# Loading the first token blocks and weights by halves in the start of a hybrid decoder layer

## The chip, the core and the metric

The kernel runs on one core of one Trainium2 chip. Its time is the device time of one execution in microseconds; lower is better. A time is given as the median of several runs, and one further execution is profiled.

## The reference

One layer of a decoder trunk on a sequence of 512 tokens, 1024 channels, in float32. Cut to what matters:

```python
u = rmsnorm(x, norm1_g)
proj = u @ w_in            # -> a_glu, q, k, v, r, g_low, gate_a, gate_b
y_conv = silu(layernorm(dwconv31(glu(a_glu)))) @ w_conv_out
y_gla = (gated_linear_attention(q, k, v, g_low) * silu(r)) @ w_gla_out
h = x + (sigmoid(gate_a) * y_conv + sigmoid(gate_b) * y_gla) @ w_o
u2 = rmsnorm(h, norm2_g)
z = dwconv3(u2 @ w_ffn_up)
h = h + (silu(z[:, :F]) * z[:, F:]) @ w_ffn_down
return rmsnorm(h, final_g)
```

The case plays in the first line and in the first product of the second one: the RMS norm of x and the first 512 of the 1024 columns of v.

## The kernel before, in words

**Products in three parts.** A float32 product is made of three products of TensorE on numbers cast to a shorter form (fp32r). Each operand is split: its high part is a cast on ScalarE, its low part is the operand less the high part, on VectorE. Of the four products of parts, the kernel makes high by high (HH), high weight by low activation (HL) and low weight by high activation (LH), and adds them up in one bank of PSUM. `mm3` (L305) does so for most of the kernel, at L309 to L311; `by_parts` (L512, product at L519) does so in the start, where the three parts can be asked for one by one.

**Tiles.** x comes in four token blocks of 128 x 1024 (x0 to x3). The weights come as blocks of 128 x 1024, 512 KB each. For v a weight block holds two steps k of the inner dimension (rows), each with 512 columns; so the first half of the columns of block w0 is step 0, its second half is step 1. A product of the start has 128 tokens of one step k as the stationary operand and the 512 columns of one half of a weight block as the moving one. One token block needs eight steps by three parts, 24 products, in one bank.

**The start (L409 to L598).** It stands under `manual_schedule`, so TensorE, ScalarE, VectorE and SyncE each do their instructions in exactly the order of the code. For the first two token blocks (`EARLY = 2`) the norm is not applied ahead of the product: `transposed` turns x to channels by tokens with four transposes per half of the columns (L433), `with_gain` multiplies by the norm's gain on VectorE (L439), `early_high` casts on ScalarE (L446) and `early_low` subtracts on VectorE (L449). The factor of each token is applied to the result (L502). `squares` (L453) sums the squares of a token block on ScalarE. The gain itself comes as `rows`, is turned by TensorE (L525) and copied by VectorE (L526). `split_weight(True)` (L259, L262) gives high and low of a weight block as two halves each, `split_weight()` (L266, L267) in one piece. `warm(n)` (L425) issues n dummy products of 128 x 128 that nobody reads; each is two instructions in the trace. `WARM` says how many stand in each of three places: before the first transposes, before the first product, and after the first six products.

**Order before the change.** SyncE issues: gain rows, x0, w0, x1, w1, w2, x2, w3, all in one piece. TensorE: 7 dummies, transposes of x0, 3 dummies, HH of block 0 on steps 0 and 1, the eight transposes of x1, HL and LH of block 0 on steps 0 and 1, 2 dummies, then HH and HL of block 0 on steps 2 and 3 (which need w1), HH of block 1 on steps 0 and 1, and so on. ScalarE casts both halves of w1 ahead of the first half of block 1. VectorE makes the gain of block 1's second half late, after the lows of w1 and of block 0's second half.

**Behind the start** (from `load_consts`, L133) the order is not written out: the framework's planner orders instructions by the order of the code, by dependencies and by its own estimates of costs, and the depthwise convolution's taps are dealt out between the products by `fill`. Weight blocks come through four buffers (`raw`, L174), each split to high and low and used by the products. The other stages are the same in both versions: GLU and convolution, attention, the merge, w_o, and the feed-forward part.

Of the kernel before, what the change touches and what calls it, by code (L numbers as in the profile page):

```python
# [10 lines left out]
F32 = mybir.dt.float32  # L11
# [6 lines left out]
P = 128  # L18
D = 1024
T = 512  # L20
# [14 lines left out]
AHEAD = 4  # L35
LOOK = 2
RATE = 5.0
WARM = (7, 3, 2)
MID = 4
EARLY = 2  # L40
PADS = (416, 2016, 640)
# [25 lines left out]
def trunk_layer(ctx: ExitStack, tc: tile.TileContext, a: dict, out: bass.AP):  # L67
    nc = tc.nc

    def pool(name, bufs, space=None):  # L70
        kw = {"space": space} if space is not None else {}
        return ctx.enter_context(tc.tile_pool(name=name, bufs=bufs, **kw))
# [10 lines left out]
    tp = pool("temps", 1)  # L83
# [8 lines left out]
    def nm(s):  # L92
        return f"{s}_{next(names)}"

    def heap(dt=F32):
        return hp.tile([P, T], dt, tag="h", name=nm("h"))
# [65 lines left out]
    ready, raws = [], []  # L162
# [4 lines left out]
    def load():  # L167
        if len(raws) < len(order):
            name, j = order[len(raws)]
            if name in SEVEN:  # L170
                raws.append(load_block(name, *j))
                return
            raw = raw_tile()
            nc.sync.dma_start(raw, a[name][j])  # L174
            raws.append(raw)

    def raw_tile():
        return wp.tile([P, D], F32, tag="raw", name=nm("raw"), bufs=4)
# [16 lines left out]
    def load_block(name, pairs, step, d):  # L195

        if step not in LOADS:
            return None
        src = block(name, pairs, d, *LOADS[step])
        n = src.shape[-1]  # L200
        if step == "a11":
            dst = keep_tile(name)[:, :n]
            kept[pairs, d] = dst
        else:
            dst = raw_tile()[:, :n]
        nc.sync.dma_start(dst, src)
        if step == "n3":
            nc.gpsimd.dma_start(dst, block(name, pairs, d, 1, 1), accum_op=ALU.add)
        if step == "n2":
            kept[pairs, d, "b22"] = dst  # L210
        return dst

    def operand(raw, pairs, step, d):

        if step == "s4":
            return kept[pairs, d, "b22"]
        if step == "n2":
            nc.vector.tensor_tensor(kept[pairs, d], kept[pairs, d], raw, ALU.add)
        return raw if step in ("a12", "n3") else kept[pairs, d]

    def sum_on(name, pairs, step, d):

        if step in ("a11", "n2"):
            nxt = block(name, pairs, d, *((0, 1) if step == "a11" else (1, 0)))
            nc.gpsimd.dma_start(kept[pairs, d], nxt, accum_op=ALU.add)

    def split_weight(halves=False, between=None):

        if len(ready) < len(order):
            while len(raws) <= len(ready):  # L230
                load()
            raw = raws[len(ready)]
            name, spec = order[len(ready)]
            if name in SEVEN:
                raw = operand(raw, *spec)
                n = raw.shape[-1]
                hi = wp.tile([P, D], F32R, tag="whi", name=nm("whi"), bufs=4)[:, :n]
                lo = wp.tile([P, D], F32R, tag="wlo", name=nm("wlo"), bufs=4)[:, :n]
                nc.scalar.copy(hi, raw)  # L239
                nc.vector.tensor_tensor(lo, raw, hi.bitcast(F32), ALU.subtract)  # L240
                sum_on(name, *spec)
                ready.append((hi, lo))
                load()
                return
            hi = wp.tile([P, D], F32R, tag="whi", name=nm("whi"), bufs=4)
            if order[len(ready)][0] == "w_low":
                nc.scalar.copy(hi, raw)
                if order[len(ready)][1] == 0:
                    part_lo = lambda t: t.rearrange("p (k c) -> p k c", c=P)[:, :, :RANK]
                    nc.vector.tensor_tensor(part_lo(hi), part_lo(raw), part_lo(hi.bitcast(F32)), ALU.subtract)  # L250
                ready.append((hi, None))
                load()
                return
            lo = wp.tile([P, D], F32R, tag="wlo", name=nm("wlo"), bufs=4)
            if halves:
                ready.append((hi, lo))

                def high(c):
                    nc.scalar.copy(hi[:, c], raw[:, c])  # L259

                def low(c):
                    nc.vector.tensor_tensor(lo[:, c], raw[:, c], hi[:, c].bitcast(F32), ALU.subtract)  # L262

                cols = [slice(j * T, (j + 1) * T) for j in range(2)]
                return [[lambda c=c, part=part: part(c) for c in cols] for part in (high, low)]
            nc.scalar.copy(hi, raw)  # L266
            pace[0] = nc.vector.tensor_tensor(lo, raw, hi.bitcast(F32), ALU.subtract)  # L267
            ready.append((hi, lo))
            load()
# [130 lines left out]
    xs, rs, xg, eu = {}, {}, {}, {}  # L400

    def load_x(t):
        xs[t] = tp.tile([P, D], F32, tag="x", name=nm("x"), bufs=3)
        nc.sync.dma_start(xs[t], a["x"][t * P : (t + 1) * P, :])

    def by_four(t):
        return t.rearrange("p (k t) -> p k t", k=4)
# [2 lines left out]
    start.__enter__()  # L410
    rows = tp.tile([P, P], F32, tag="gain", name=nm("rows"), bufs=1)[0:KT, :]
    nc.sync.dma_start(rows, a["norm1_g"].rearrange("(k p) -> k p", p=P))
    load_x(0)
    load()
    load_x(1)
    load()
    load()
    load_x(2)
# [17 lines left out]
    def with_gain(tr, g):  # L436
        f = heap()
        by_channel = gains[:, g * 4 : g * 4 + 4].unsqueeze(2).to_broadcast([P, 4, P])
        nc.vector.tensor_tensor(by_four(f), by_four(tr), by_channel, ALU.mult)  # L439
        return f  # L440
# [4 lines left out]
    def high(hi, f):  # L445
        nc.scalar.copy(hi, f)  # L446

    def low(lo, f, hi):
        nc.vector.tensor_tensor(lo, f, hi.bitcast(F32), ALU.subtract)  # L449
# [16 lines left out]
    def early_gain(t, g):  # L466
        xg[t, g] = with_gain(xg[t, g], g)
        eu[t, g] = [by_four(heap(F32R)) for _ in range(2)]

    def early_high(t, g):  # L470
        high(eu[t, g][0], by_four(xg[t, g]))

    def early_low(t, g):
        low(eu[t, g][1], by_four(xg[t, g]), eu[t, g][0])
# [35 lines left out]
    HH, HL, LH = (0, 0), (0, 1), (1, 0)  # L510

    def by_parts(acc, t, ks, parts=(HH, HL, LH)):  # L512

        for wi, ai in parts:
            for k in ks:
                act = eu[t, k // 4][ai][:, k % 4, :] if t < EARLY else acts1[k][ai][:, t * P : (t + 1) * P]
                j = slice((k % 2) * T, (k % 2 + 1) * T)
                first, last = k == 0 and (wi, ai) == HH, k == KT - 1 and (wi, ai) == LH
                nc.tensor.matmul(acc, act, ready[k // 2][wi][:, j], start=first, stop=last)  # L519

    accs = [mm_bank() for _ in range(EARLY)]
    warm(WARM[0])
    xg[0, 0] = transposed(xs[0], 0)
# [6 lines left out]
    highs, lows = split_weight(True)  # L530
    highs[0]()
    early_high(0, 0)
    highs[1]()
    warm(WARM[1])
    lows[0]()
    early_low(0, 0)
    lows[1]()
    by_parts(accs[0], 0, (0, 1), (HH,))
    early_acts(1)
    squares(0)  # L540
    by_parts(accs[0], 0, (0, 1), (HL, LH))
    warm(WARM[2])
    early_gain(1, 0)
    highs, lows = split_weight(True)
    for half in (*highs, *lows):
        half()
    early_high(1, 0)
    load()
    early_low(1, 0)
    early_high(0, 1)  # L550
    by_parts(accs[0], 0, (2, 3), (HH, HL))
    by_parts(accs[1], 1, (0, 1), (HH,))
    by_parts(accs[0], 0, (2, 3), (LH,))
    by_parts(accs[1], 1, (0, 1), (HL, LH))
    by_parts(accs[1], 1, (2, 3))
    early_low(0, 1)
    early_gain(1, 1)
    split_weight()
    load_x(3)
    early_high(1, 1)  # L560
# [54 lines left out]
    for k in range(KT):  # L615
# [4 lines left out]
        c = heap()  # L620
# [504 lines left out]
    class Finish:  # L1125
# [8 lines left out]
        def part(self, n, c):  # L1134
            hn = hres[self.t, n][:, c]
            k = len(self.parts)
            nc.scalar.activation(junk(T)[:, c], hn, AF.Square, scale=1.0 / 32.0, accum_out=self.ss[:, k : k + 1])
            y = self.y[:, n * T + c.start : n * T + c.stop] if self.y else tmp() if self.parts else hn
            nc.vector.tensor_tensor(y, hn, gain3[:, n * T + c.start : n * T + c.stop], ALU.mult)
            self.parts.append((n, y))  # L1140
            self.width += c.stop - c.start
            if k == 0:
                self.sum = small(1, "var")
                nc.vector.tensor_scalar(self.sum, self.ss[:, 0:1], EPS, None, ALU.add)
            elif self.width < D:
                nc.vector.tensor_tensor(self.sum, self.sum, self.ss[:, k : k + 1], ALU.add)
# [39 lines left out]
    for gi, pairs in enumerate(GROUPS):  # L1186
        acts = []
        early = {}
        if gi == 0:

            ws = [weight("w_up", j, 0) for i in pairs[0] for j in (i, FT + i)]
            accs = [mm_bank() for _ in ws]
# [107 lines left out]
```

## Time and profile before

| | |
|---|---|
| median of 3 runs | 838.51 us (837.78 to 838.71) |
| the profiled execution's own time | 837.74 us |
| its span | 836.0 us |
| instructions | 10033 |
| moved by DMA | 97.79 MB, mean 117 GB/s |

The profile is of one execution. Its span is counted from the first instruction to the last; the time of an execution holds a little more, here 1.74 us. Times in the views are counted from the start of the span. A row of a timeline has start, length, engine, line, operation, what is written and read, and a count; in brackets stands how long the engine sat idle before and what ended it. PE is TensorE, PEld its weight load, ACT ScalarE, DVE VectorE, POOL GpSimd, SP SyncE. The matmuls are pipelined, so neighbouring rows of PE overlap. The tiles in the start: `x` token blocks, `raw` weight blocks, `whi` and `wlo` their high and low parts, `h` both the gained activations and their parts, `ax` the bank of transposes, `mm` the banks of products.

### The profile page before, as it was taken

To read this page: it belongs to the slowest core of one execution; us is meant where nothing else is said; L and a number is where in the kernel's file an instruction comes from. 1 tells how busy PE (TensorE), PEld (TensorE's weight loads), DVE (VectorE), ACT (ScalarE), POOL (GpSimd) and SP (SyncE) were. 2 spreads that over 40 slices of the span, in tenths; PEclk is the share of its full clock that TensorE was granted. 3 is DMA by queue.
4 is the path that set the end of the run, shared out by engine and by line. 5 is a ranking of instruction groups with operands and counts; after the bars stand their busy time and mean duration, and the time that the engine had idled before them with its cause. 6 is when DMAs were issued, how large, how long until landed. Compare 5 with 4: busy or idle time off the path is not lost.

```text
span 836.0 us, 10033 instructions
## 1 busy us (share of the span) xinstructions
PE 826.9 (99%) x3845; PEld 691.3 (83%) x3845; DVE 650.3 (78%) x927; ACT 388.0 (46%) x541; POOL 42.8 (5%) x64
## 2 busy tenths in 40 slices
PE   9999999999999999999999999999999999999996
PEld 7888888888888888888888898888888888888885
DVE  6689979999998798744689858778757787676795
ACT  6633247445543422449444635444434444444454
POOL 2000000000100100000001100001000010000111
PEclk9999999999999999999999999999999999999999
DMA  8232232222222322232348634234842238222462
GB/s 312 102 102 101 101 104 80 101 76 96 82 76 76 127 100 101 76 102 75 114 89 237 190 128 142 88 98 102 217 148 89 69 86 286 102 91 87 101 125 102
DMA packets 28593, 97.79 MB, mean 117 GB/s; under 512 B 3240, under 2 KB 3632, under 8 KB 28544
## 3 DMA queue, kind: packets, MB, share of 16 engines
q1 hardware_dynamic: 25088, 85.35, 29.2%
q0 software_dynamic: 3456, 11.80, 8.1%
q8 instruction: 30, 0.49, 0.2%
q14 instruction: 19, 0.16, 0.1%
HBM read 95.03 MB, written 2.10 MB: 116 GB/s over the span
## 4 chain that ended last, share of the span: by engine, by line
PE 96%; DVE 1%; DMA 1%; issue 0%; ACT 0%; POOL 0%; SPq 0%; POOLq 0%; ACTq 0%
PE mm L309 29%; PE mm L310 29%; PE mm L311 29%; PE mm L519 3%; PE ax L854 1%; PE ax L310 1%; PE ax L309 1%; PE ax L311 1%; DMA x<-in_x_dram 1%; PE ax L856 1%; PE ax L836 1%; PE ax L823 0%; PE ax L871 0%; DVE hres L1019 0%; PE ax L822 0%; PE ax L433 0%
## 5 line engine op out<-in xcount | busy, mean ns | idle before, releaser
L309 PE MATMUL mm<-uh,wlo 128*128 128x512 f32 (+1 forms) x768 | 294.8, 384 | 0.0
L311 PE MATMUL mm<-uh,whi 128*128 128x512 f32 (+1 forms) x768 | 292.4, 381 | 0.0
L310 PE MATMUL mm<-ul,whi 128*128 128x512 f32 (+1 forms) x768 | 292.2, 380 | 0.0
L266 ACT CAST whi<-raw 128x1024 fp32r<-128x1024 f32 x114 | 118.7, 1046 | 129.0 <-PE mm L311 97.2
L311 PEld LDWEIGHTS mm<-uh,whi 128*128 128x128 f32 x768 | 144.4, 188 | 27.8
L309 PEld LDWEIGHTS mm<-uh,wlo 128*128 128x128 f32 x768 | 144.5, 188 | 27.0
L310 PEld LDWEIGHTS mm<-ul,whi 128*128 128x128 f32 x768 | 144.5, 188 | 26.9
L267 DVE TENSOR_TENSOR wlo<-raw,whi 128x1024 fp32r<-128x1024 f32 x114 | 138.3, 1217 | 34.9 <-ACT whi L266 34.8
L613 DVE SCALAR_TENSOR_TENSOR c<-h,pp,c 128x511 f32<-128x511 f32 (+14 forms) x240 | 162.3, 727 | 0.7
L1083 DVE SCALAR_TENSOR_TENSOR tmp<-mm,pp,tmp 128x511 f32<-128x511 f32 x88 | 65.8, 748 | 68.1 <-ACT tmp L1081 67.0
L1081 ACT ACTIVATE tmp<-mm,pp 128x512 f32<-128x512 f32 x44 | 34.3, 780 | 62.6 <-PE mm L311 62.6
L239 ACT CAST whi<-kept 128x1024 fp32r<-128x1024 f32 (+1 forms) x32 | 31.7, 994 | 21.7 <-PE mm L311 9.7
L240 DVE TENSOR_TENSOR wlo<-kept,whi 128x1024 fp32r<-128x1024 f32 (+1 forms) x32 | 36.6, 1152 | 2.5 <-ACT whi L239 2.3
L1019 DVE TENSOR_TENSOR hres<-hres,mm 128x512 f32<-128x512 f32 (+1 forms) x49 | 32.7, 671 | 3.3 <-PE mm L311 2.7
L239 ACT CAST whi<-raw 128x1024 fp32r<-128x1024 f32 (+1 forms) x24 | 23.7, 995 | 20.2 <-PE mm L311 18.7
L240 DVE TENSOR_TENSOR wlo<-raw,whi 128x1024 fp32r<-128x1024 f32 (+1 forms) x24 | 27.3, 1152 | 3.9 <-ACT whi L239 3.8
L310 PE MATMUL mm<-wlo,sh 128*128 128x512 f32 x66 | 25.8, 391 | 0.0
L311 PE MATMUL mm<-whi,sh 128*128 128x512 f32 x66 | 25.7, 389 | 0.0
L309 PE MATMUL mm<-whi,sl 128*128 128x512 f32 x66 | 25.5, 389 | 0.0
L309 PE MATMUL mm<-h,wlo 128*128 128x512 f32 x64 | 25.4, 397 | 0.0
L310 PE MATMUL mm<-h,whi 128*128 128x512 f32 x64 | 24.9, 389 | 0.0
L311 PE MATMUL mm<-h,whi 128*128 128x512 f32 x64 | 24.9, 389 | 0.0
(251 smaller groups left out, 1122.3 us busy)
## 6 DMA issues: line engine op xcount, KB each, us to landing
raw<-in_w_up_dram SPq DMA_DIRECT2D x44, 512.0 KB, 3.5
raw<-in_w_glu_dram SPq DMA_DIRECT2D x16, 512.0 KB, 3.9
raw<-in_w_down_dram SPq DMA_DIRECT2D x15, 512.0 KB, 3.2
kept<-in_w_down_dram POOLq DMA_DIRECT2D x10, 512.0 KB, 5.2
raw<-in_w_v_dram SPq DMA_DIRECT2D x8, 512.0 KB, 3.7
raw<-in_w_qk_dram SPq DMA_DIRECT2D x8, 512.0 KB, 3.2
raw<-in_w_r_dram SPq DMA_DIRECT2D x8, 512.0 KB, 3.3
raw<-in_w_gb_dram SPq DMA_DIRECT2D x8, 512.0 KB, 3.2
```

The source lines that it names most:

```text
L239: nc.scalar.copy(hi, raw)
L240: nc.vector.tensor_tensor(lo, raw, hi.bitcast(F32), ALU.subtract)
L266: nc.scalar.copy(hi, raw)
L267: pace[0] = nc.vector.tensor_tensor(lo, raw, hi.bitcast(F32), ALU.subtract)
L309: nc.tensor.matmul(acc, ll, rh, start=first, stop=False, **kw)
L310: nc.tensor.matmul(acc, lh, rl, start=False, stop=False, **kw)
L311: nc.tensor.matmul(acc, lh, rh, start=False, stop=last, **kw)
L519: nc.tensor.matmul(acc, act, ready[k // 2][wi][:, j], start=first, stop=last)
L613: nc.vector.scalar_tensor_tensor(y[:, s:], c[:, : T - s], w, y[:, s:], ALU.mult, ALU.add)
L1019: nc.vector.tensor_tensor(hres[t, n][:, c], hres[t, n][:, c], bank[of[step]][i][:, c], op)
L1081: nc.scalar.activation(z, acc, AF.Identity, bias=pp[:, PP_FB + m : PP_FB + m + 1], scale=w[2])
L1083: nc.vector.scalar_tensor_tensor(z[:, s:], acc[:, : T - s], w[j], z[:, s:], ALU.mult, ALU.add)
```

## The change

The diff:

```diff
-WARM = (7, 3, 2)
+WARM = (5, 2, 2)
...
-    load_x(0)
-    load()
-    load_x(1)
+
+    raws.append(raw_tile())
+    for t in range(EARLY):
+        xs[t] = tp.tile([P, D], F32, tag="x", name=nm("x"), bufs=3)
+    for t, c in ((t, slice(j * T, (j + 1) * T)) for t in range(EARLY) for j in range(2)):
+        nc.sync.dma_start(xs[t][:, c], a["x"][t * P : (t + 1) * P, c])
+        if t == 0:
+            nc.sync.dma_start(raws[0][:, c], a["w_v"][0][:, c])
     load()
     load()
     load_x(2)
...
     warm(WARM[1])
-    lows[0]()
     early_low(0, 0)
-    lows[1]()
+    for half in lows:
+        half()
     by_parts(accs[0], 0, (0, 1), (HH,))
     early_acts(1)
     squares(0)
     by_parts(accs[0], 0, (0, 1), (HL, LH))
     warm(WARM[2])
     early_gain(1, 0)
+    early_gain(1, 1)
+    early_high(1, 0)
+    early_low(1, 0)
     highs, lows = split_weight(True)
     for half in (*highs, *lows):
         half()
-    early_high(1, 0)
     load()
-    early_low(1, 0)
     early_high(0, 1)
+    by_parts(accs[1], 1, (0, 1), (HH,))
     by_parts(accs[0], 0, (2, 3), (HH, HL))
-    by_parts(accs[1], 1, (0, 1), (HH,))
+    by_parts(accs[1], 1, (0, 1), (HL, LH))
     by_parts(accs[0], 0, (2, 3), (LH,))
-    by_parts(accs[1], 1, (0, 1), (HL, LH))
     by_parts(accs[1], 1, (2, 3))
     early_low(0, 1)
-    early_gain(1, 1)
     split_weight()
```

SyncE now issues x0, w0 and x1 as six transfers of half the columns each (256 KB, rows of 2 KB): first half of x0, first half of w0, second half of x0, second half of w0, then the two halves of x1; behind them w1, w2, x2 and w3 in one piece as before. In the prediction a and b stand for the first and second half (x1b is the second half of x1). The dummies become 5, 2 and 2. On VectorE the low part of block 0's first half goes ahead of both lows of w0; both gains and the first low of block 1 go ahead of the lows of w1. On ScalarE the cast of block 1's first half goes ahead of both casts of w1. On TensorE the HH of block 1 on steps 0 and 1 comes before the products of block 0 on steps 2 and 3, and its HL and LH come before block 0's LH on steps 2 and 3. The same products are made, and the same bytes are loaded.

## The prediction

> **What bounds the kernel now.** I read the page first: the span, the busy shares and the chain that ended last.
>
> ```profile
> span 836.0 us, 10033 instructions
> ...
> PE 826.9 (99%) x3845; PEld 691.3 (83%) x3845; DVE 650.3 (78%) x927; ACT 388.0 (46%) x541; POOL 42.8 (5%) x64
> ...
> PE 96%; DVE 1%; DMA 1%; issue 0%; ACT 0%; POOL 0%; SPq 0%; POOLq 0%; ACTq 0%
> ```
>
> TensorE is busy for 826.9 of 836.0 us and carries 96% of the chain. So nothing but TensorE time counts, and only 9.1 us of it are idle. The next view, busy time by stretches, says where those 9.1 us are not:
>
> ```profile
> 33.39:825.00 791.61, 791.56 (x3663) 661.73 (x3662) 622.75 (x880) 361.48 (x497) 36.55 (x42) 1.00 0.37 114
> ```
>
> From 33.39 us, where the hand-ordered start ends, to 825 us TensorE is busy for 791.56 of 791.61 us. Whatever the start saves or loses is handed through to the end undiminished, and nothing behind it can be won. The question is at which time TensorE's unbroken work begins. The chain of waits over the first 40 us answers it (columns: start, length, what):
>
> ```profile
> 2.13 6.11 DMA x<-in_x_dram
> 8.28 1.09 PE ax L433 x8
> 9.38 0.93 PE mm L519 x4
> 10.31 0.44 PE mm L425 x4
> 10.75 6.92 PE mm L519 x30
> ...
> 25.38 8.18 PE mm L519 x36
> ```
>
> The end of the kernel hangs on the landing of the second token block at 2.13 + 6.11 = 8.24 us. From there TensorE does that block's eight transposes (1.09 us), four products (0.93), four dummy products (0.44), and from 10.75 on products without a break: 6.92/30 = 0.231 us each, later 8.18/36 = 0.227. Before the landing TensorE has room to spare, as its timeline shows:
>
> ```profile
> 1.12 3.32 PE L425 MATMUL mm<-ones 128*128 128x128 f32 x14 [1.12 <-DVE ones L398]
> 4.70 0.63 PE L433 MATMUL ax<-ident,x 128*128 128x128 f32 x4 [0.26 <-DMA x<-in_x_dram]
> ...
> 5.90 0.83 PE L425 MATMUL mm<-ones 128*128 128x128 f32 x6
> 7.11 1.02 PE L519 MATMUL mm<-whi,h 128*128 128x512 f32 x2 [0.38 <-ACT h L446]
> 8.28 1.09 PE L433 MATMUL ax<-ident,x 128*128 128x128 f32 x8
> ```
>
> Each dummy of the code is two instructions. The first product starts at 7.11 us and two are done by 8.1; after that TensorE sits until x1 is there. So the time of the first product is not what the end hangs on; x1 is.
>
> **The change, part by part.**
>
> *Loads by halves.* Five transfers of 512 KB (x0, w0, x1 among them) become two whole ones and six halves of 256 KB. What does a half cost? Four rows: the page's landing times, and the packets of stretches that hold one lone transfer each (one of 256 KB in 2.0 us, one of 512 KB in 2.5 us):
>
> ```profile
> raw<-in_w_down_dram SPq DMA_DIRECT2D x15, 512.0 KB, 3.2
> raw<-in_w_down_dram SPq DMA_DIRECT2D x3, 256.0 KB, 2.5
> ```
> ```profile
> q1 hardware_dynamic: 144, 0.26, 36.6%
> ```
> ```profile
> q1 hardware_dynamic: 144, 0.52, 60.7%
> ```
>
> A lone half lands 0.7 us sooner. Its packets take 0.366 x 16 x 2.0 = 11.7 us of engine time, two halves 23.4; the whole takes 0.607 x 16 x 2.5 = 24.3. So two halves take the engines no longer than one whole. The halves cost more on SyncE's queue, which issues them one by one:
>
> ```profile
> 1.26 0.36 SPq L404 DMA_DIRECT2D x<-in_x_dram  x1
> 1.67 0.42 SPq L174 DMA_DIRECT2D raw<-in_w_v_dram  x1
> 2.13 0.43 SPq L404 DMA_DIRECT2D x<-in_x_dram  x1
> 2.60 1.01 SPq L174 DMA_DIRECT2D raw<-in_w_v_dram  x2
> ```
> ```profile
> x<-in_x_dram SPq DMA_DIRECT2D x1, 512.0 KB, 3.3
> raw<-in_w_v_dram SPq DMA_DIRECT2D x1, 512.0 KB, 4.1
> ```
>
> x0 is issued at 1.26 and lands 3.3 later, at 4.6; w0 is issued at 1.67 and lands 4.1 later, at 5.8. With 0.46 us per issue (2.13 to 2.60 and on), the order x0a, w0a, x0b, w0b, x1a, x1b puts x1's second half at 1.26 + 5 x 0.46 = 3.6 us instead of 2.13, and w1 at 4.0 instead of 2.60; everything behind them on SyncE (w2, x2, w3) is 1.4 us later too. At 3.6 us, however, four halves are still on their way: I put x0a at 1.26 + 2.5 = 3.8 us, then one half per 0.7 us, w0a 4.5, x0b 5.2, w0b 5.9 (the whole w0 was 5.8). The engines do not run dry, so x1 is complete when as many bytes as before have come: 8.24 us. Bounds: an earlier landing down to 7.3 (the spacing of 0.7 continued), and a later one by the whole delay of its issue, 1.4 us. I take 0.15 us later, near the equal-engine-time rows, for more semaphore packets and the later issue. x1a comes between, at about 7.0 to 7.6.
>
> *Fewer dummies (14 to 10 instructions, 6 to 4, 4 unchanged).* They lie before x1's landing, where TensorE waits; removing them gains nothing there. The first run ends at 1.12 + 10 x 0.237 = 3.5 us instead of 4.4.
>
> *x0's way to the first product.* From the transposes at 4.70 to the product at 7.11 are 2.4 us: transposes, two steps on VectorE, one on ScalarE.
>
> ```profile
> 5.72 1.29 DVE L439 TENSOR_TENSOR h<-ax,gains 128x512 f32<-128x512 f32 x2
> 6.92 0.68 DVE L262 TENSOR_TENSOR wlo<-raw,whi 128x512 fp32r<-128x512 f32 x1
> 7.52 0.68 DVE L449 TENSOR_TENSOR h<-h,h 128x512 fp32r<-128x512 f32 x1
> 8.12 0.68 DVE L262 TENSOR_TENSOR wlo<-raw,whi 128x512 fp32r<-128x512 f32 x1
> 8.98 0.69 DVE L439 TENSOR_TENSOR h<-ax,gains 128x512 f32<-128x512 f32 x1 [0.17 <-PE ax L433]
> ```
> ```profile
> 6.44 0.62 ACT L446 CAST h<-h 128x512 fp32r<-128x512 f32 x1
> 6.97 0.62 ACT L259 CAST whi<-raw 128x512 fp32r<-128x512 f32 x1
> 7.49 1.05 ACT L453 ACTIVATE junk<-x 128x1024 bf16<-128x1024 f32 x1
> 8.45 0.19 ACT L453 ACTIVATION_READ_ACCUMULATOR junk<-x 128x1 f32 x1
> 9.58 1.14 ACT L259 CAST whi<-raw 128x512 fp32r<-128x512 f32 x2 [0.95 <-DMA raw<-in_w_v_dram]
> ```
>
> Starting at 3.8 the first product comes at about 6.3, 0.8 sooner. That is worth nothing by itself, as TensorE then waits for x1. It lets VectorE be ahead: two gains, then three lows (0.6 us from start to start), from 4.9 to 8.3 at the latest, so the gains of x1 run from 8.3 to 9.5 and ScalarE's cast of x1's first half is done by about 9.7.
>
> *x1's transposes.* Four of the eight now run on x1a, before x1b has landed. Behind the landing stand four: 1.09/2 = 0.54 us less. This is the main term.
>
> *New order of the products.* Behind x1: 0.54 + 0.93 + 0.44 from 8.28 gives 10.19 us. The first products of block 1 come next, ahead of those of w1. They need the cast of 9.7, which is there. Before, the next product needed w1, whose cast starts at 9.58 and lets its first product run at 10.2. Now two (then four more) products of block 1 cover 0.45 us, and w1's casts, which stand behind block 1's on ScalarE, end at 9.7 + 0.57 = 10.3 and 10.9; the products on them are due at 10.65 and 10.88. So the new wait is about 0.05 us, and what is queued behind it on TensorE (the LH and HL parts) waits as long. Cost of the reorder if w1 lands 0.5 later: up to 0.4 us.
>
> *Later blocks.* w2's cast and low, in the trace:
>
> ```profile
> 11.67 1.05 ACT L266 CAST whi<-raw 128x1024 fp32r<-128x1024 f32 x1
> ```
> ```profile
> 13.25 1.22 DVE L267 TENSOR_TENSOR wlo<-raw,whi 128x1024 fp32r<-128x1024 f32 x1
> ```
>
> With 18 products from 10.19 on, w2's are due at 14.3, its low at 15.2. The low ended at 14.47; it may slip 0.7 before it is felt.
>
> **Sum:** 0.55 (10.75 to 10.19) less 0.15 for x1b = 0.4 us. The profiled execution took 837.74 us (span 836.0 and 1.74 around it), and would take 837.3. It lies 0.77 under the median of the runs shown, 838.51; from the median the forecast is **838.1**. Its own range is 837.6 to 838.4.
>
> **Rivals.**
>
> *The clock stays at half (slower).* In the trace a dummy takes 3.32/14 = 0.237 us up to 4.4 us and 0.44/4 = 0.11 at 10.31: TensorE starts at half speed and is at full speed after some 3 us of nearly unbroken dummies. The change cuts them to 2.4 us and leaves a gap of about 0.4 us before x0a. If full speed comes only by 8.2 us, it costs nothing, as TensorE waits then anyway; that landing is the point from which it decides. Each microsecond of half speed behind it loses half. Full speed at 11 us: 1.4 less the 0.4, 839.5; at 14.5 us: 3.1 less 0.4, 841.2. For it: two fewer of seven dummies. Against: the gap is short, and much work follows it.
>
> [...]
>
> *x1 lands sooner.* Should x1b land at 7.3, VectorE binds: the cast of block 1 at 9.7 is the earliest for its first product, against 10.75: 1.05 us with the dummies swallowed in the wait, some 0.9 after the hand-over from engine to engine, 837.6. For it: halves of 0.7 us. Against: the whole x1 came 2.4 us behind w0, and byte counts do not change.
>
> *The change does not do what it says.* x1b lands 0.5 later by its later issue, or w1's casts, pushed behind block 1's, eat the gain: 838.5.
>
> *The work behind the start is arranged anew.* Orders behind 33 us are made by a planner; a shift in the start may change them. With 0.05 us idle in 791.61 this can only cost: a wait put onto TensorE costs about one VectorE step, 0.7 to 1.2 us (the rows above); one of them is lost in the runs' scatter, three to four would give some 840.5 to 842.
>
> **Chances.** Forecast 0.52; x1 sooner 0.12; no gain 0.14; half clock to about 11 us 0.07, to about 14.5 us 0.07; rearranged 0.08. The range of 837.1 to 839.6 takes in the first four and leaves out the longest half clock and the rearranged, 0.15, and the edge of the second. A measurement of this kernel can tell about 0.2%, 1.7 us, from no change, and most cases lie inside it: same 0.81 (0.52 + 0.08 + 0.14 + 0.07); slower 0.15 (0.07 + 0.08); faster 0.04, the part of x1 sooner that the scatter of the runs (837.78 to 838.71 before) can carry past it.
>
> **What would show it.** Right: x1's second half lands within 0.3 us of 8.24; four transposes, not eight, stand behind it in the chain; unbroken products begin near 10.2 to 10.4; the first product at about 6.3. Wrong: dummies or transposes of 0.2 us spacing after 8 us (clock); a wait of TensorE for ScalarE's cast of w1 of over 0.2 us; x1b beyond 8.6; idle time of TensorE beyond 33 us.

## The result and the profile after

The changed kernel takes 840.4 us (median of 8 runs, 839.51 to 842.33), the kernel before 838.25 us beside it (8 runs, 837.69 to 838.85). The medians lie 2.15 us apart; the ratio worked out from all runs is 1.0029, 95% interval 1.002 to 1.0039: slower by 1.7 to 3.3 us, about 2.4. The forecast of 838.1 was wrong in sign, and the time lies outside its range. The profiled execution of after took 840.14 us.

The page of after, span and busy shares (they answer to 836.0 and 826.9):

```profile
span 838.4 us, 10026 instructions
...
PE 827.5 (99%) x3839; PEld 691.6 (82%) x3839; DVE 650.4 (78%) x927; ACT 387.9 (46%) x541; POOL 42.7 (5%) x64
```

And busy time by stretches of after, over a stretch of the same length as the one of before, begun 2.4 us later:

```profile
35.79:827.40 791.61, 791.55 (x3663) 661.41 (x3662) 622.56 (x880) 361.22 (x497) 36.48 (x42) 1.00 0.38 114
```

Behind the start TensorE is as full as before, with the same 3663 matmuls. The whole loss was made in the start and handed through. The chain of waits of after (start, length, what):

```profile
2.13 5.39 DMA x<-in_x_dram
...
7.57 1.11 PE ax L438 x4
8.68 0.85 PE mm L430 x4
9.54 0.85 PE mm L524 x2
10.39 1.17 PE ax L438 x8
11.56 0.93 PE mm L524 x4
12.49 0.45 PE mm L430 x4
12.94 7.11 PE mm L524 x30
```

Before, the chain passed through the landing of x1 at 8.24 us. Now it passes through the second half of **x0**, which lands at 2.13 + 5.39 = 7.52 us; forecast was 5.2. The unbroken products begin at 12.94 instead of 10.75, 2.19 us later, and the 30 products take 7.11 instead of 6.92, 0.19 more. Together that is the 2.4 us between the spans.

Two more things are to be read in these rows. Four dummy instructions take 0.85 us at 8.68 and 0.45 at 12.49, two products 0.85 us at 9.54 and four 0.93 at 11.56: TensorE runs at half speed until about 10 or 11 us. Before, it was at full speed from the transposes at 4.70 on (four in 0.63 us, against 1.08 for the first four of after, at 4.03). And all eight transposes of x1 stand in the chain, none of them ahead.

Busy time by stretches of before and after, the same five microseconds (last two columns: DMA share and GB/s). Before:

```profile
3.00:4.00 1.00, 1.00 (x6) 1.00 (x6) 0.00 (x0) 0.00 (x0) 0.23 (x1) 1.00 1.06 389
4.00:5.00 1.00, 0.74 (x6) 0.51 (x5) 0.00 (x0) 0.00 (x0) 0.00 (x0) 1.00 0.99 373
5.00:6.00 1.00, 1.00 (x9) 0.81 (x8) 0.45 (x2) 0.21 (x1) 0.00 (x0) 1.00 1.11 250
6.00:7.00 1.00, 0.74 (x7) 0.54 (x5) 1.00 (x3) 0.97 (x3) 0.00 (x0) 1.00 0.87 340
7.00:8.00 1.00, 0.86 (x2) 0.37 (x2) 1.00 (x3) 1.00 (x3) 0.00 (x0) 1.00 1.02 393
```

After:

```profile
3.00:4.00 1.00, 0.62 (x3) 0.33 (x3) 0.00 (x0) 0.00 (x0) 0.25 (x1) 1.00 1.04 275
4.00:5.00 1.00, 0.97 (x4) 0.71 (x4) 0.00 (x0) 0.00 (x0) 0.00 (x0) 1.00 0.54 168
5.00:6.00 1.00, 0.31 (x2) 0.18 (x1) 0.62 (x2) 0.61 (x1) 0.00 (x0) 1.00 0.91 260
6.00:7.00 1.00, 0.00 (x0) 0.00 (x0) 0.24 (x1) 0.62 (x2) 0.00 (x0) 1.00 1.00 279
7.00:8.00 1.00, 0.43 (x2) 0.43 (x3) 0.00 (x0) 0.00 (x0) 0.00 (x0) 1.00 0.65 209
```

The sum over the five is 1.75 MB before and 1.19 MB after. All six halves were issued by 4 us, w1 and w2 by 5.3, and yet the DMA engines stand idle for up to half of a microsecond (share 0.54, 0.65). The halves of x1 are issued at 3.08 and about half of the row's 0.91 us later, near 3.54, as SyncE's row shows, and the DMA view of after, over the stretch of 3.4 to 3.9 us, says that they land 5.9 us later (the median of the two):

```profile
3.08 0.91 SPq L418 DMA_DIRECT2D x<-in_x_dram  x2
```
```profile
x<-in_x_dram SPq DMA_DIRECT2D x2, 256.0 KB, 5.9
```

So x1 is complete at about 9.5 us instead of 8.24. The last view of after is VectorE's timeline:

```profile
5.55 0.69 DVE L444 TENSOR_TENSOR h<-ax,gains 128x512 f32<-128x512 f32 x1
8.72 0.69 DVE L444 TENSOR_TENSOR h<-ax,gains 128x512 f32<-128x512 f32 x1 [2.48 <-PE ax L438]
9.33 0.68 DVE L454 TENSOR_TENSOR h<-h,h 128x512 fp32r<-128x512 f32 x1
9.93 1.29 DVE L262 TENSOR_TENSOR wlo<-raw,whi 128x512 fp32r<-128x512 f32 x2
11.16 1.29 DVE L444 TENSOR_TENSOR h<-ax,gains 128x512 f32<-128x512 f32 x2
```

Between the two gains of x0 VectorE idles for 2.48 us, though the low part of x0's first half (at 9.33) had its operands since 6.9. It stands behind the second gain in an order written by hand, and that gain waits for x0's second half. Everything behind it moves along: three lows, then the gains of x1, then ScalarE's cast of x1's first half, which ends at 12.5 us (11.89 and 0.62 long) where the forecast had 9.7.

Three causes are therefore possible: the loads, the dummies (clock), and the order with its wait on VectorE.

### The profile page after: what moved, and what is told of

Same layout as the page of the kernel before. It is cut to its first block, busy times and chain, and to the rows that moved or that the text cites. A ratio compares the mean times of both kernels' runs of the same rounds, so it can differ in the third digit from the quotient of the medians.

```text
span 838.4 us, 10026 instructions
## 1 busy us (share of the span) xinstructions
PE 827.5 (99%) x3839; PEld 691.6 (82%) x3839; DVE 650.4 (78%) x927; ACT 387.9 (46%) x541; POOL 42.7 (5%) x64
## 4 chain that ended last, share of the span: by engine, by line
PE 96%; DVE 1%; DMA 1%; issue 0%; ACT 0%; POOL 0%; SPq 0%; POOLq 0%; ACTq 0%
PE mm L311 29%; PE mm L310 29%; PE mm L309 29%; PE mm L524 3%; PE ax L859 1%; PE ax L311 1%; PE ax L310 1%; PE ax L309 1%; DMA x<-in_x_dram 1%; PE ax L861 1%; PE ax L841 1%; PE ax L438 0%; PE ax L828 0%; DVE hres L1024 0%; PE ax L876 0%; PE ax L827 0%
```

## The experiments

Theory 1: two causes, slow halves and a late clock. Rivals: the halves alone (2), the dummies alone (3), the order has a share (4). The times below are ratios to the kernel before, run on the same chip; 0.1% is 0.84 us.

**One part at a time.** The first kernel has the dummies alone.

```diff
-WARM = (7, 3, 2)
+WARM = (5, 2, 2)
```

> The kernel before, with the dummies of the change alone (5, 2, 2). Theory 1, two causes: the shorter first run of dummies leaves TensorE at half speed past the landing of x1, and the halves arrive slower; here only the first acts, so +0.8 to +1.5 us against the kernel before, full speed at about 7.7 or 10.9 us instead of 4.3. Theory 2, the loads are the whole cause (the clock stays at half only because TensorE waits so long for the second half of x0): within 0.2 us of the kernel before, full speed before 8.2 us. Theory 3, the dummies are the whole cause: +2.0 us or more.

Measured: 838.93 us, ratio 1.0008 (0.9999 to 1.0016). Theory 3 falls. The chain of waits of its profile shows half speed until after 10 us:

```profile
9.04 1.71 PE ax L433 x8
10.74 0.92 PE mm L519 x4
```

Eight transposes take 1.71 us instead of 1.09, four products 0.92 as before. Over the runs the loss is 0.7 us at the ratio, with zero just inside the interval, so theories 1 and 2 are not told apart here.

The second has the halves alone, all else as before:

```diff
-    load_x(0)
-    load()
-    load_x(1)
+    raws.append(raw_tile())
...
+    for t, c in ((t, slice(j * T, (j + 1) * T)) for t in range(EARLY) for j in range(2)):
+        nc.sync.dma_start(xs[t][:, c], a["x"][t * P : (t + 1) * P, c])
+        if t == 0:
+            nc.sync.dma_start(raws[0][:, c], a["w_v"][0][:, c])
```

> The kernel before, with the loads by halves alone; dummies and order as before. Theory 1 (two causes): the second half of x1 lands at 9.2 to 9.6 us instead of 8.24, and the time is +0.7 to +1.3 us with full speed by 4.5 us. Theory 2 (loads alone): +1.8 to +2.4 us, full speed at about 10.9 us as in the changed kernel. Theory 3 (dummies alone): within 0.2 us of the kernel before, or up to 0.5 us faster, the second half of x1 at 8.3.

Measured: 839.88 us, ratio 1.0019 (1.0008 to 1.003), +0.7 to +2.5 us. Two of its stretches show the same slow loads and idle engines (0.63), in another execution and with seven dummies:

```profile
4.00:5.00 1.00, 1.00 (x7) 0.93 (x5) 0.00 (x0) 0.00 (x0) 0.00 (x0) 1.00 1.10 176
5.00:6.00 1.00, 0.53 (x3) 0.18 (x1) 0.40 (x2) 0.00 (x0) 0.00 (x0) 1.00 0.63 195
```

The third has the order alone: of the diff of the change, the part from `warm(WARM[1])` on, with whole loads and dummies 7, 3, 2.

> The kernel before, with the new order of products, casts and lows alone; whole loads, dummies 7, 3, 2. Theories 1, 2 and 3: the order costs nothing, 0 to -0.3 us. Theory 4, the order has a share in the loss (the casts of w1 stand behind those of block 1): +0.3 us or more, and TensorE waits for ScalarE's cast of w1 by 0.3 us or more.

Measured: 838.43 us, ratio 1.0004 (0.9996 to 1.0013). No effect that can be told. The wait that theory 4 spoke of is there, the loss is not shown: TensorE's weight loads wait twice for the cast of w1, which now stands behind that of block 1, 0.22 and 0.34 us.

```profile
11.12 0.19 PEld L520 LDWEIGHTS mm<-whi,h 128*128 128x128 f32 x1 [0.22 <-ACT whi L259]
11.65 0.99 PEld L520 LDWEIGHTS mm<-whi,h 128*128 128x128 f32 x5 [0.34 <-ACT whi L259]
```

The fourth is the change with the old dummies:

```diff
-WARM = (5, 2, 2)
+WARM = (7, 3, 2)
```

> The changed kernel with the dummies of before (7, 3, 2). Theory 1 (two causes): full speed at about 4.3 us, +0.3 to +1.0 us against the kernel before, 1.2 to 1.6 less than the changed kernel. Theory 2 (loads alone): +1.8 to +2.4 us, as the changed kernel. Theory 3 (dummies alone): -0.5 to 0 us.

Measured: 840.19 us, ratio 1.0022 (1.0014 to 1.0031). A saving by the old dummies cannot be told (the interval of the change is 1.002 to 1.0039): theory 2 fits, theory 1 had put the clock's share too high. The profiled execution was the fastest of its runs (838.25 us), so its profile says little of the median. It does show other landings than the profile of the change: x0's second half was there 4.0 us after its issue, at 6.1 (5.4 us, at 7.5, in the change), and its chain passes through the second half of w0, at 7.5.

**Which loads are slow, and when.** The same kernel as the fourth, but halves of 64 partitions with whole rows:

```diff
-        nc.sync.dma_start(xs[t][:, c], a["x"][t * P : (t + 1) * P, c])
+        nc.sync.dma_start(xs[t][c, :], a["x"][t * P + c.start : t * P + c.stop, :])
```

(c being the 64 partitions; w0 likewise.)

> As the changed kernel with dummies 7, 3, 2, but each half is 64 partitions with their whole rows of 4 KB, in the same order and the same number of transfers. Theory A, the pieces of 2 KB out of rows of 4 KB are slow to read: x1 is complete at 8.1 to 8.5 us, DMA moves 350 GB/s or more between 3 and 8 us, and the time is 0 to +0.5 us against the kernel before. Theory B, the greater number of transfers in flight is slow: x1 complete at 8.8 us or later and +1.5 to +2.2 us, as the changed kernel with dummies 7, 3, 2.

Measured: 842.27 us, ratio 1.0051 (1.0039 to 1.0064). Slower still, so long rows alone are no cure. From 3 to 9 us its DMA moves 205 to 262 GB/s with the engines busy nearly all the time (share 0.89 to 1.08), which is a different picture from the idle engines of the column halves. As a test of theory A against B it fails: 64 partitions have a cost of their own.

Next, x0, x1 and w0 were laid out by halves in memory, each half 256 KB without gaps:

```diff
+        "x_halves": i["x"][0][: EARLY * P].reshape(EARLY, P, 2, T).transpose(0, 2, 1, 3),
+        "w_v_halves": _rows(w_in, (C_V, C_V + T))[0].reshape(P, 2, T).transpose(1, 0, 2),
```

> As the changed kernel with dummies 7, 3, 2, but x0, x1 and w0 stand in memory by halves, so that each half is read from one unbroken 256 KB (rows of 2 KB, one behind the other). Theory A1, the gaps between the pieces are what is slow (only every other 2 KB is read at a time): x1 complete by 8.4 us, -0.5 to +0.3 us against the kernel before. Theory A2, any packet of 2 KB is slow when the queue is full: x1 complete at 8.8 us or later, +1.5 to +2.2 us. Theory B (number of transfers): as A2.

Measured: 838.93 us, ratio 1.0009 (1.0 to 1.0018). It lies between the two theories: 0.13%, 1.1 us, less than with gaps. The gaps have a share, by these ratios a little over half of the loss; it isn't shown beyond doubt, as the intervals of the two kernels (1.0014 to 1.0031 and 1.0 to 1.0018) overlap in a narrow stretch.

Then the transfers by themselves, 4 MB of each kind in a burst, twice; each burst begins when the one before has landed. The kinds, for block j and half c:

```diff
+        nc.sync.dma_start(big[:, j, :], w[j])
...
+        nc.sync.dma_start(big[:, j, halves[c]], w[j][:, halves[c]])
...
+        nc.sync.dma_start(big[:, j, halves[c]], w[j].rearrange("(h p) (c d) -> h (p c) d", h=2, c=2)[c])
...
+        nc.sync.dma_start(big[r, j, :], w[j][r, :])
```

> The rest of the computation is left out: only transfers of 4 MB each are timed, one kind after another, the five kinds twice (whole blocks of 512 KB; halves of the columns, a then b of one block; halves of the columns of two blocks in turn, as the change does; unbroken halves of 256 KB; halves of 64 partitions). Theory A1, gaps between pieces: whole and unbroken halves at 380 GB/s or more, both kinds of column halves at 280 GB/s or less. Theory A2, packets of 2 KB are slow in themselves: all three kinds of 2 KB at 280 or less, 64 partitions fast. Theory C, column halves are slow in the first microseconds alone (long packets at a cold start): all three kinds of 2 KB at 350 GB/s or more here. Halves of 64 partitions: 200 to 260 GB/s, as in the run before.

Stretches of that run: whole blocks (the last two columns are again DMA share and GB/s),

```profile
1.50:2.50 1.00, 0.42 (x1) 0.00 (x0) 1.00 0.71 139
2.50:3.50 1.00, 0.00 (x0) 0.00 (x0) 1.00 1.02 406
3.50:4.50 1.00, 0.00 (x0) 0.00 (x0) 1.00 1.03 414
```

halves of the columns, a then b of one block, from the burst's beginning near 14 us,

```profile
14.00:16.00 2.00, 0.10 (x1) 0.00 (x0) 1.00 0.70 223
16.00:18.00 2.00, 0.00 (x0) 0.00 (x0) 1.00 0.95 277
18.00:20.00 2.00, 0.00 (x0) 0.00 (x0) 1.00 0.80 247
20.00:22.00 2.00, 0.00 (x0) 0.00 (x0) 1.00 1.01 350
22.00:24.00 2.00, 0.00 (x0) 0.00 (x0) 1.00 1.04 402
```

and unbroken halves, from near 121 us:

```profile
121.00:123.00 2.00, 0.00 (x0) 0.00 (x0) 1.00 0.92 240
123.00:125.00 2.00, 0.00 (x0) 0.00 (x0) 1.00 1.00 360
```

None of the three theories holds as put. A long stream of column halves reaches 402 GB/s, no worse than whole blocks (419 from 6.5 to 12 us) by more than a few per cent. But whole blocks move 406 GB/s from 2.5 to 3.5 us and 369 to 419 behind that, while column halves move 223 to 277 for six microseconds first, in part with idle engines (0.80; the 0.70 holds the wait for the first bytes as well). The second burst of the column halves does the same (250, 240, 286, then 360 and 408), against 328, 385 and 412 in the second burst of whole blocks. The stretches shown differ in length and in where they begin. Over six microseconds from about the first bytes on, the two bursts of each kind move 359 and 375 GB/s (whole blocks), 301 and 297 (unbroken halves), 271 and 258 (column halves), and 264 and 245 (a fifth kind: column halves of two blocks in turn). So by this count about two thirds of the shortfall come with halves even without gaps, and a third with the gaps; the run does not tell the number of transfers from the shorter rows. The start of this kernel is just such a burst, and six microseconds at 245 to 271 GB/s move 1.47 to 1.63 MB: its six halves, 1.57 MB, lie in the slow part.

**The forecast's main term by itself.** Only x1 by halves, x0 and w0 whole, the new order, dummies 7, 3, 2; against the third kernel:

```diff
-    load_x(1)
+    xs[1] = tp.tile([P, D], F32, tag="x", name=nm("x"), bufs=3)
+    for c in (slice(j * T, (j + 1) * T) for j in range(2)):
+        nc.sync.dma_start(xs[1][:, c], a["x"][P : 2 * P, c])
```

> x0 and w0 whole, only x1 in two halves of its columns, the new order, dummies 7, 3, 2. The gain that was forecast (four transposes of x1 ahead of its second half) stands alone here. If it is real where loads are not slowed before it: the second half of x1 at 8.2 to 8.6 us, -0.5 to 0 us against the new order with whole loads. If column halves are slow whichever they are: the second half at 8.9 or later, +0.3 to +1 us.

Measured: 838.72 us, ratio 1.0012 (1.0003 to 1.0021), against 1.0004 of the third kernel. No gain here either. In its profile x1's halves, issued at 2.13 and 2.60, landed 5.1 us later, by 7.8 us, and still the chain holds eight transposes:

```profile
8.35 0.85 PE mm L522 x2
9.21 1.46 PE ax L436 x8
```

The two products before them end at 9.2. The transposes stand behind these products in TensorE's order, so having x1's first half early does not let four of them run early. That execution was also at half speed here (0.85 us for the two products), with seven dummies. In the third kernel's profile, at full speed by then (the eight transposes behind them take 0.97 us), the same two products end at 8.45 us, which is later than 7.8 too.

**The clock.** The fourth kernel with eight more dummies between the two transposes of x0:

```diff
+    warm(8)
     xg[0, 1] = transposed(xs[0], 1)
```

> The changed kernel with dummies 7, 3, 2 and 8 more between the two transposes of x0, where TensorE waits for the second half of x0. If half speed of TensorE during or after that wait is a share of the loss with halves: 0.5 to 1.2 us less than without the 8, +0.7 to +1.3 us against the kernel before. If the late landings are all of it: within 0.3 us of the run without them, +1.5 to +2.2 us.

Measured: 839.86 us, ratio 1.0023 (1.0013 to 1.0032). TensorE is at full speed from the first transposes on (four in 0.46 us; the 8 dummies are 16 instructions in 2.05 us, 0.13 each, in its chain), and the loss cannot be told from the fourth kernel's. What then binds is VectorE; its chain of waits:

```profile
7.23 0.65 PE ax L438 x4
...
8.51 0.68 DVE h L454
9.20 1.20 DVE wlo L262 x2
10.40 0.61 DVE h L444
...
11.04 0.63 ACT h L451
...
11.71 1.02 PE mm L524 x3
```

From x0's second half through the second gain, the low, the two lows of w0 and the gain of x1 to the cast of block 1, and only then TensorE's products of block 1.

The changed kernel with whole loads (order and dummies 5, 2, 2 stay), which is the third kernel with the dummies of the change:

```diff
-WARM = (7, 3, 2)
+WARM = (5, 2, 2)
```

> The changed kernel with whole loads of x0, w0, x1: new order and dummies 5, 2, 2 stay. If loads are the larger cause and the dummies the smaller: +0.7 to +1.2 us against the kernel before, 1.0 to 1.4 less than the changed kernel. If dummies and order are the larger: +1.5 us or more.

Measured: 838.62 us, ratio 1.0005 (0.9996 to 1.0014). Whole loads alone take 0.24% of the 0.29% away; the loss that is left cannot be told from none.

Last, the kernel before without its first seven dummies:

```diff
-WARM = (7, 3, 2)
+WARM = (0, 3, 2)
```

> The kernel before without the first seven dummies (0, 3, 2): whole loads, old order. It bounds what the clock can cost here. If half speed behind x1's landing is paid for as reckoned (half of the time from 8.2 us to full speed): full speed at 10.5 to 11.5 us in nearly every execution, +1.2 to +1.7 us against the kernel before, and more than with five dummies (+0.9 us there). If the clock's price is small because other engines bind in that stretch: +0.3 to +0.9 us.

Measured: 839.03 us, ratio 1.001 (1.0001 to 1.0019). That bounds what all seven first dummies are worth: 0.1 to 1.6 us. The middle, 0.8 us, fits the second expectation; the interval still reaches into the first, from 1.2 on. That lacking all seven costs more than the three fewer dummies of the first kernel is not shown.

**A try at something better.** Whole loads in the order x0, x1, w0, all transposes ahead of the first product, dummies 7, 10, 0; the heart of it:

```diff
     load_x(0)
-    load()
     load_x(1)
+    load()
...
+    early_acts(1)
...
+    warm(WARM[1])
+    highs, lows = split_weight(True)
...
+    for part in (HH, HL, LH):
+        for t in range(EARLY):
+            by_parts(accs[t], t, (0, 1), (part,))
```

> The kernel before with whole loads in the order x0, x1, w0; all transposes before the first product, then both blocks on steps 0 and 1, dummies 7, 10, 0. If the wait for the third 512 KB is what the front hangs on (all theories): the third one lands at 8.2 us as before, but behind it stands only a cast, not eight transposes; the unbroken products begin at about 8.9 us with none made, against 10.75 with six made (six take 1.36), so -0.3 to -0.6 us against the kernel before. If the clock or the casts of w0 and w1 on ScalarE bind instead: 0 to +0.5 us.

Measured: 838.99 us, ratio 1.0013 (1.0004 to 1.0021): a miss. In its chain ScalarE casts block 1 until 8.97 us and w0's first half only from 8.99 on, and the first product comes at 9.66 instead of 8.9; the wait behind the third transfer was not the only one. No kernel of the study beats the one before.

## Why the prediction was wrong

*What bounds the kernel: right.* TensorE is the bound, the start is handed through undiminished (791.55 of 791.61 us busy), and nothing behind it changed. The rival of a rearranged rest did not come true.

*Loads by halves: this step failed.* It is the term of 0.15 us for x1b, and the landings that it rests on. The text said that "the engines do not run dry, so x1 is complete when as many bytes as before have come", and took 0.15 us. The engines did run dry (share 0.54 and 0.65), the bytes of 3 to 8 us fell from 1.75 to 1.19 MB, x1 was complete at about 9.5 us, 1.2 later than before, and x0 at 7.5 instead of 5.2. The two price rows were lone transfers on an idle queue; they give engine time per byte, and that was right (a long stream of halves goes at 402 GB/s). They say nothing on how a burst begins. The run of loads alone shows that it begins at 223 to 277 GB/s for six microseconds. One row of before would have been nearer, a burst of eight column halves of x later in the kernel, in the DMA view:

```profile
hres<-in_x_dram SPq DMA_DIRECT2D x8, 256.0 KB, 7.4
```

Its 7.4 us to landing, against 2.5 for a lone half, was there to be read. Other transfers share that stretch, so it is no clean price, but it could have served as an upper bound. Nearest came the rival in which the change does not do what it says: it has x1b late, but by 0.5 us, and no loss.

*x0's way to the first product: failed through the same landing.* It was called worth nothing because TensorE waits for x1. It became the path: with x0's second half at 7.5 us, VectorE's gain of it holds back the low that was ready, two lows of w0 and the gains of x1. The text listed the three lows behind the two gains, but with x0's second half put at 5.2 us it saw no wait in the second gain; with x0 in one piece both gains were ready together, and the wait was none. The products on steps 0 and 1 do not read x0's second half at all: its transposes and its gain stand ahead of them by the order of the code alone. The profiles of the five kernels with x0 in halves of its columns fit this path, though they differ in order and dummies as well. The half landed at 7.5 us in the change, 7.6 with the halves alone, 7.1 with dummies between, 6.5 with unbroken halves and 6.1 in the fastest run of the fourth kernel; their spans are 838.4, 838.1, 837.8, 837.2 and 836.5 us, against 836.0 before. No run moves that gain behind the lows, so what the order on VectorE costs by itself is not shown.

*x1's transposes: the main term, 0.54 us, did not exist.* They stand behind the HH of block 0 in TensorE's order, and those products came at 9.2 to 10.2 us. So x1's landing at 9.5, late as it was, did not bind either. Even with x1 whole by 7.8 us (x1 by halves alone) all eight stood in the chain.

*New order: mis-sized.* A wait of 0.05 us for w1's cast was forecast; 0.22 and 0.34 us came with the order alone, whose effect of 1.0004 is not to be told from none. In the change itself TensorE's weight loads wait 0.33 us for that cast, at 13.6.

*The clock: the mechanism was rightly a rival, its price too high.* In the profile of after half speed lasted past 10 us. It was priced at half of the time behind 8.2 us, 1.4 us. Measured with whole loads: 0.7 us (interval -0.1 to 1.3) for three dummies fewer, 0.1 to 1.6 us for the first seven. With halves the runs with all dummies of before, and with eight more, lose about as much as the change (1.0022 and 1.0023 against 1.0029, in overlapping intervals). In the profiled execution block 1's cast, at the end of VectorE's chain, is done at 12.5 us and the unbroken products begin at 12.94; full speed could have won at most 0.4 us there. At the head of that chain the four transposes of x0's second half take 1.11 us, against 0.65 at full speed with the dummies between: by these rows, an estimate of 0.5 us more.

Half speed lasted past 7 us in all three profiles with five first dummies: four dummy instructions take 0.85 us at 8.68 in the change, at 7.14 with the dummies alone and at 7.07 with whole loads, against 0.44 at 10.31 before. As far as matmuls show it, it did so in one of the nine with seven too (x1 by halves alone, six in 1.28 us at 7.07), so the number of dummies seems to shift the odds and settles no single execution. The 14.5 us of that rival's longer case were the author's estimate; in the profile of the change four products take 0.93 us from 11.56 on, full speed, which is near the 11 us of its shorter case.

The parts one at a time give 0.08 + 0.19 + 0.04 = 0.31% beside the 0.29% of the change. Only the halves are shown to lose by themselves; for dummies and for order alone zero lies inside the interval. What stays open: how the remaining 0.05 to 0.1% divides between dummies and order, how the halves' loss divides between late landings and the order on VectorE, and what in the DMA path makes a burst of halves begin slowly. The run of loads alone shows when and how much, not why.

## What to carry to other kernels

In this case a transfer's price had two parts: its share of a steady stream, and how it behaves at the beginning of a burst. Price the loads of a kernel's start from a burst in the trace, not from a lone transfer. And where an order is written by hand, ask of each wait what ready work stands behind it on the same engine: cutting an operand in two gains only if the second half's wait does not block what the first half already allows.

## What the runs showed of the hardware

Halves of 64 partitions are slow in themselves: in the run of loads alone they move 229 to 274 GB/s from 136 to 144 us with the engines fully busy (whole blocks 385 to 424 from 81 to 89 us); two stretches of this second burst:

```profile
136.00:138.00 2.00, 0.00 (x0) 0.00 (x0) 1.00 1.01 274
138.00:140.00 2.00, 0.00 (x0) 0.00 (x0) 1.00 1.03 234
```

In one profile full speed, once reached, was lost within the start. In the kernel with halves of 64 partitions TensorE has no busy time from 5 to 7 us, starts six instructions in 0.76 us behind that, and then the granted clock (third column from the right) falls to 0.53; eight transposes take 1.71 us at 12.16, against 1.09 before. What made it fall is not shown.

```profile
7.00:8.00 1.00, 0.76 (x6) 0.60 (x6) 0.00 (x0) 0.00 (x0) 0.00 (x0) 1.00 1.08 246
8.00:9.00 1.00, 1.00 (x6) 1.00 (x6) 0.86 (x2) 0.64 (x1) 0.00 (x0) 0.53 1.01 234
```

The same column reads 1.00 from 3 to 4 us before and after, where dummies of 0.24 us (before) or 0.25 (after) against 0.11 later show half speed: at the beginning of these traces the spacing of equal instructions is the better clock.
